# Combining two contraction tiles at a time: 512 KB loads and 512-wide vector steps beside a saturated TensorE

## The chip, the core and the metric

The kernel runs on one core of a Trainium2 chip. The metric is the time of one execution in device microseconds. TensorE does the matrix products (PE in the rows, its weight loads PEld), VectorE (DVE) and ScalarE (ACT) do elementwise work, GpSimd (POOL) issues the loads that add into their target, and SyncE (SP) issues nearly all other loads, in one queue that is worked off in order. Each engine executes its own list of instructions strictly in order.

## The reference

A decoder trunk of two layers over 512 tokens with 1024 features in float32. Each layer is, cut to what matters here:

```python
h = rmsnorm(x, norm_g)
proj = h @ w_in                      # feeds four token mixers, their gates and merge_in
...
merge = merge_in.reshape(B, T, N_BRANCH, D_MODEL)
for i, o in enumerate((o_nsa, o_pool, o_conv, o_fox)):
    branch = (o * silu(gates[:, :, i])) @ w_branch[i]
    acc += sigmoid(merge[:, :, i]) * branch
x = x + acc @ w_out
```

## The kernel before

Every float32 operand is split into a high and a low part in a reduced float32 format (`split`, line 69: ACT writes the high part, DVE subtracts it for the low part), and a product is three matmuls: high by high, low by high, high by low. Weights come as tiles of 128x1024 (512 KB); SP loads them one after the other into a small number of slots, `Stream` (line 97) hands them out in one fixed order, and `split` turns a tile into `wh` and `wl`, of which there are two buffers each. A `dense` (line 283) is one such tile against all eight tiles of the normed input: 24 matmuls.

A layer goes through these stages: projections, then attention (twelve units of four query blocks, with `dense` work between them to fill PE), then `branches(m)` for m = 0 to 3, each followed by four `dense` that compute merge logits (dense A to D of that `m` in this text), then `merge`, then the output projection. The merge logits of the other half of the features are computed in `merge` by a scheme with seven products in place of eight (`PRODUCTS`): the product of the two halves of the contraction and the two halves of the tokens is formed from combinations of the blocks. The combined weights are added up by accumulating loads and DVE. The combined inputs are made by `combine_h` (line 850) from x, which is read again from DRAM: the quarter pairs of contraction tile k and k + 4 are loaded, scaled by the norm's gain on ACT (line 867), and combined on DVE into P7, P6 and P3, which are then split. `combine_h` is a generator. Its steps are taken one at a time from within the dense work after the branches (lines 1218 to 1230), and the rest of it at the product P7 in `merge`.

Three buffers matter. `ptc` (2 buffers of 128x512) first holds the compressed probabilities of the attention, and then the x tiles of `combine_h`. `rope` (1 buffer of 128x2x512) holds the rotary tables and then two decay rows of the attention; from `more` (line 137) on it is one more slot for a merge weight, beside three slots cut from the attention's value tile `V` and the three ordinary `wr` slots.

The program order above is not the final one: when the kernel is built, a scheduler of the language reorders the instructions of each engine, by its own model of how long things take. So `combine_h` starts in the middle of the attention, and a change in one place moves instructions in others.

Of the kernel before, what the change touches and what calls it, by code (L numbers as in the profile page):

```python
# [9 lines left out]
F32R = mybir.dt.float32r  # L10
AF = mybir.ActivationFunctionType
ALU = mybir.AluOpType
# [4 lines left out]
T = 512  # L17
# [27 lines left out]
def trunk_kernel(ctx: ExitStack, tc: tile.TileContext, xT, w_all, par_all, const, gains, rope, outT):  # L45
    nc = tc.nc
    PE, ACT, DVE, POOL = nc.tensor, nc.scalar, nc.vector, nc.gpsimd
# [9 lines left out]
    def sb(shape, tag, bufs, dt=F32):  # L57
        return work.tile(shape, dt, tag=tag, name=tag, bufs=bufs)

    def temp():  # L60
        return sb([128, T], "t", 8)

    def psum(tag, bufs):
        return ps.tile([128, T], F32, tag=tag, name="ps_" + tag, bufs=bufs)
# [4 lines left out]
    def split(hi, lo, src, scale=None):  # L69

        if scale is None:
            ACT.activation(hi, src, AF.Copy)  # L72
            DVE.tensor_tensor(lo, src, f32(hi), ALU.subtract)  # L73
        else:
            ACT.activation(hi, src, AF.Copy, scale=scale)  # L75
            DVE.scalar_tensor_tensor(lo, src, scale, f32(hi), op0=ALU.mult, op1=ALU.subtract)  # L76
# [4 lines left out]
    ng = cpool.tile([128, 24], F32, name="ng")  # L81
# [11 lines left out]
    class Stream:  # L93
# [43 lines left out]
        def more(self):  # L137

            big = sb([128, 3, 1024], "V", 1)
            self.slots += ["rope"] + [big[:, n] for n in range(3)]  # L140
            self.fill()

        def next_raw(self):
# [73 lines left out]
    ws = Stream()  # L217
# [36 lines left out]
    def stats(n=T, keep=False):  # L254
        sum_squares(n, False, True)
        p = state["ssq"]
        nt = n // 128
        rt = sb([128, 4], "rtok", 2)
        DVE.tensor_scalar(rt[:, :nt], p[:, 0:nt], 1.0 / DM, 1e-6, op0=ALU.mult, op1=ALU.add)
        POOL.tensor_tensor(rt[:, :nt], rt[:, :nt], nhalf[:, :nt], ALU.pow)  # L260
        p2 = psum("o", 1)
        for tt in range(nt):
            PE.matmul(p2[:, tt * 128:tt * 128 + 128], rt[:, tt:tt + 1].to_broadcast([128, 128]), ident,
                      start=(tt == 0), stop=(tt == nt - 1))
        if keep:
            return rt, p2
        rb = sb([128, T], "rstd", 1)
        ACT.activation(rb, p2, AF.Copy)
        return rt, rb
# [220 lines left out]
    def cmp_attention():  # L490
        kc, vc, q, g = state["kc"], state["vc"], state["nq"], state["g"]
        pc = sb([128, 4, 4, 32], "p", 5)
        flat = pc.rearrange("p a h n -> p (a h) n")
        for half in range(2):
            p = psum("s", 2)
            for j in range(8):
                qt, h = half * 2 + j // 4, j % 4
                PE.matmul(p[:, j * 64:j * 64 + 64], q[h][:, qt * 128:qt * 128 + 128], kc,
                          start=(j == 0), stop=(j == 7))
            pv = p.rearrange("p (j two n) -> p j two n", two=2, n=32)  # L500
            t = temp()
            tv = t[:, 0:256].rearrange("p (j n) -> p j n", n=32)
            ACT.activation(tv, pv[:, :, 1, :], AF.Copy)
            yield
            DVE.tensor_tensor(flat[:, half * 8:half * 8 + 8, :], pv[:, :, 0, :], tv, ALU.add)
            yield
        for qt in range(4):
            m = cst[:, C_CM + qt * 32:C_CM + qt * 32 + 32].rearrange("p (o n) -> p o n", o=1)
            DVE.tensor_tensor(pc[:, qt], pc[:, qt], m.to_broadcast([128, 4, 32]), ALU.add)
        yield  # L510
        nm, sm = sb([128, 16], "cnm", 1), sb([128, 16], "csm", 1)
        DVE.tensor_reduce(nm, flat, axis=AX.X, op=ALU.min)

        def bc(a):
            return a.rearrange("p (a o) -> p a o", o=1).to_broadcast([128, 16, 32])

        yield
        DVE.tensor_tensor(flat, flat, bc(nm), ALU.subtract)
        ACT.activation(flat, flat, AF.Exp, scale=-1.0)
        yield  # L520
        DVE.tensor_reduce(sm, flat, axis=AX.X, op=ALU.add)
        DVE.reciprocal(sm, sm)
        DVE.tensor_tensor(sm.rearrange("p (a h) -> p a h", h=4), sm.rearrange("p (a h) -> p a h", h=4),
                          g[:, :, 0:4], ALU.mult)
        DVE.tensor_scalar(sm[:, 0:4], sm[:, 0:4], cst[:, C_VAL:C_VAL + 1], None, op0=ALU.mult)
        DVE.tensor_tensor(flat, flat, bc(sm), ALU.mult)
        yield
        yield
        pt = psum("pt", 2)
        for qt in range(4):  # L530
            PE.transpose(pt[:, qt * 128:qt * 128 + 128], pc[:, qt].rearrange("p h n -> p (h n)"), ident)
        ph, pl = sb([128, T], "ptc", 2, F32R), sb([128, T], "ptc", 2, F32R)
        split(ph, pl, pt)
        state["pc"] = (ph, pl)
        yield
# [314 lines left out]
    def combine_h(l):  # L850

        src = xT.rearrange("(k p) t -> k p t", p=128) if l == 0 else x1d
        H = T // 2
        S = state["S"] = {n: [] for n in ("P7", "P6", "P5", "P3")}
        lo_, hi_ = slice(0, H), slice(H, T)
        keep = []
        for k in range(4):
            xa = [sb([128, T], "ptc", 2) for _ in range(2)]
            for n in range(2):
                nc.sync.dma_start(xa[n], src[k + 4 * n])  # L860
            if k % 2 == 0:
                pair = {n: [sb([128, 2, H], "st", 20, F32R) for _ in range(2)] for n in ("P7", "P6", "P3")}
                s1 = sb([128, 2, H], "p", 5)
                keep.append(s1)
            yield
            for n in range(2):
                ACT.activation(xa[n], xa[n], AF.Copy, scale=ng[:, 8 * l + k + 4 * n:8 * l + k + 4 * n + 1])
            yield
            c = k % 2
            tmp = sb([128, 2, H], "p", 5)  # L870

            def parts(name, t):
                h, lo = (x[:, c] for x in pair[name])
                split(h, lo, t)
                S[name].append((h, lo))

            DVE.tensor_tensor(tmp[:, 0], xa[0][:, lo_], xa[0][:, hi_], ALU.subtract)
            DVE.tensor_tensor(s1[:, c], xa[1][:, hi_], xa[0][:, hi_], ALU.subtract)
            parts("P7", tmp[:, 0])
            yield  # L880
            DVE.scalar_tensor_tensor(tmp[:, 1], s1[:, c], -1.0, xa[0][:, lo_], op0=ALU.mult, op1=ALU.subtract)
            parts("P6", tmp[:, 1])
            yield
            s4 = xa[1][:, lo_]
            DVE.scalar_tensor_tensor(s4, s4, -1.0, tmp[:, 1], op0=ALU.mult, op1=ALU.subtract)
            parts("P3", s4)
            yield

        for k in range(4):
            h, lo = xh[k][:, hi_], xl[k][:, hi_]  # L890
            split(h, lo, keep[k // 2][:, k % 2])
            S["P5"].append((h, lo))
            yield
# [163 lines left out]
    for k in range(KT):  # L1057
        t = temp()
# [31 lines left out]
    for l in range(L):  # L1090
# [97 lines left out]

        fill = filler()
        side = itertools.chain(decay(l), cmp_attention())  # L1190
        for n in range(48):
            next(fill)
# [23 lines left out]

        ah, al = [], []
        side = combine_h(l)
        steps = 20
        for m in range(4):  # L1220
            if m == 1:
                ws.more()
# [62 lines left out]
    for half in range(2):  # L1285
        c = slice(half * T // 2, half * T // 2 + T // 2)
# [3 lines left out]
        _, rb = stats(T // 2, keep=True)  # L1290
        x = xn[KT - 1][:, c]
# [3 lines left out]
        for m in range(KT):  # L1295
            x = xn[m][:, c]
# [134 lines left out]
```

## Time and profile before

| what | value |
|---|---|
| median of 3 runs | 954.5 us (954.34 to 955.58) |
| profiled execution | 954.59 us, its span 952.8 us |
| TensorE busy | 933.3 us, 98% of the span |
| VectorE busy | 714.3 us, 75% |
| ScalarE busy | 520.2 us, 55% |
| mean DMA rate | 131 GB/s |

The profiled execution's time is 1.8 us more than its span, which goes from the first to the last instruction in the trace. Busy shares are averages over stages. The granted TensorE clock was 0.998 of full speed over the run, so the clock plays no part here.

### The profile page before, as it was taken

The numbers are of one execution on the slowest core, as the hardware profiler recorded it, in microseconds if no ns is written. First come the engines' busy times: TensorE is split into PE (matmuls) and PEld (weight loads), VectorE is DVE, ScalarE is ACT, GpSimd is POOL, SyncE is SP. The second block draws the span as 40 slices with busy tenths as digits, with TensorE's granted clock in tenths as the row PEclk, the third lists the DMA queues.
The fourth block names the chain that finished last, engine by engine and source line by source line (L and its number), as shares of the span: only waits on it lengthen the run. The fifth ranks groups of instructions, "written<-read, shape, count | busy, mean of one in ns | idle before, by whom it ended". The sixth has DMA issues, their size and how long they took to land.

```text
span 952.8 us, 12820 instructions
## 1 busy us (share of the span) xinstructions
PE 933.3 (98%) x4680; PEld 792.0 (83%) x4680; DVE 714.3 (75%) x1392; ACT 520.2 (55%) x906; POOL 31.1 (3%) x45
## 2 busy tenths in 40 slices
PE   7999999999999999999999999999999999999996
PEld 5988888888877888887889888888888788888796
DVE  6695689986887977776668548999777887686765
ACT  6295475575545454544426636656665455546273
POOL 0000000000000000000000000000000000010002
PEclk9999999999999999999999999999999999999999
DMA  6253122222136667643515421221322566685353
GB/s 267 79 161 127 67 89 67 79 89 89 67 122 167 176 202 217 177 155 130 192 64 162 142 89 67 89 67 47 110 67 78 179 166 187 198 208 199 112 166 122
DMA packets 39614, 124.73 MB, mean 131 GB/s; under 512 B 4464, under 2 KB 6528, under 8 KB 39552
## 3 DMA queue, kind: packets, MB, share of 16 engines
q1 hardware_dynamic: 35712, 112.38, 35.8%
q0 software_dynamic: 2976, 10.50, 5.7%
q10 hardware_dynamic: 864, 1.05, 0.3%
q8 instruction: 36, 0.59, 0.3%
q14 instruction: 26, 0.21, 0.1%
HBM read 119.72 MB, written 4.19 MB: 130 GB/s over the span
## 4 chain that ended last, share of the span: by engine, by line
PE 96%; DVE 2%; ACT 1%; DMA 1%; issue 0%; POOL 0%; DVEq 0%; SPq 0%; ACTq 0%; POOLq 0%
PE ps_d L303 56%; PE ps_d L988 9%; PE ps_s L988 5%; PE ps_o L698 3%; PE ps_pt L676 3%; PE ps_pt L988 2%; PE ps_pt L1026 2%; PE ps_s L554 2%; PE ps_pt L554 2%; PE ps_s L832 2%; PE ps_s L653 2%; PE ps_s L652 1%; PE ps_pt L832 1%; PE ps_o L1026 1%; PE ps_d L1026 1%; PE ps_o L415 1%
## 5 line engine op out<-in xcount | busy, mean ns | idle before, releaser
L303 PE MATMUL ps_d<-xh,wh 128*128 128x512 f32 x632 | 250.3, 397 | 9.0 <-ACT xh L75 6.8
L303 PE MATMUL ps_d<-xl,wh 128*128 128x512 f32 x632 | 250.2, 396 | 0.0
L72 ACT ACTIVATE wh<-wr 128x1024 fp32r<-128x1024 f32 (+2 forms) x134 | 138.9, 1038 | 155.2 <-PE ps_d L303 71.5
L73 DVE TENSOR_TENSOR wl<-wr,wh 128x1024 fp32r<-128x1024 f32 (+2 forms) x134 | 160.4, 1199 | 54.1 <-ACT wh L72 52.2
L303 PE MATMUL ps_d<-xh,wl 128*128 128x512 f32 x632 | 174.1, 392 | 0.0
L303 PEld LDWEIGHTS ps_d<-xh,wh 128*128 128x128 f32 x632 | 119.9, 190 | 32.9 <-ACT xh L75 6.8
L303 PEld LDWEIGHTS ps_d<-xl,wh 128*128 128x128 f32 x632 | 119.5, 189 | 23.8 <-DVE xl L76 1.2
L303 PEld LDWEIGHTS ps_d<-xh,wl 128*128 128x128 f32 x632 | 117.5, 188 | 23.1
L657 ACT ACTIVATE p<-p,nm 128x128 f32<-128x128 f32 (+1 forms) x96 | 53.3, 556 | 35.4 <-DVE nm L655 35.2
L324 DVE TENSOR_TENSOR t<-ps_d,rstd 128x512 f32<-128x512 f32 x74 | 50.7, 686 | 26.7 <-PE ps_d L303 26.3
L655 DVE CUSTOM_DVE_ANT_0 p<-ps_s,cst 128x128 f32<-128x128 f32 (+1 forms) x96 | 45.6, 484 | 13.0 <-PE ps_s L653 6.8
L72 ACT ACTIVATE ptx<-ps_pt 128x384 fp32r<-128x384 f32 (+1 forms) x72 | 37.0, 522 | 23.2 <-PE ps_o L698 14.4
L698 PE MATMUL ps_o<-ptx,V 128*128 128x256 f32 (+1 forms) x288 | 48.8, 282 | 0.6 <-DVE ptx L73 0.6
L698 PEld LDWEIGHTS ps_o<-ptx,V 128*128 128x128 f32 x288 | 42.4, 190 | 3.6 <-DVE ptx L73 0.8
L73 DVE TENSOR_TENSOR ptx<-ps_pt,ptx 128x384 fp32r<-128x384 f32 (+1 forms) x72 | 42.0, 593 | 2.1 <-ACT ptx L72 2.0
L676 PE MATMUL ps_pt<-cst,p 128*128 128x128 f32 x240 | 40.1, 276 | 0.0
L303 PE MATMUL ps_d<-y,wh 128*128 128x256 f32 (+1 forms) x176 | 38.0, 336 | 0.9 <-ACT y L75 0.9
L303 PE MATMUL ps_d<-st,wh 128*128 128x256 f32 (+1 forms) x176 | 33.5, 332 | 0.0
L72 ACT ACTIVATE wh<-V 128x1024 fp32r<-128x1024 f32 x18 | 19.1, 1061 | 22.7 <-PE ps_s L832 7.2
L303 PEld LDWEIGHTS ps_d<-y,wh 128*128 128x128 f32 x176 | 27.9, 190 | 4.2 <-ACT y L75 1.4
L73 DVE TENSOR_TENSOR wl<-V,wh 128x1024 fp32r<-128x1024 f32 x18 | 22.0, 1223 | 12.5 <-ACT wh L72 12.5
L676 PEld LDWEIGHTS ps_pt<-cst,p 128*128 128x128 f32 x240 | 28.1, 140 | 3.3
(341 smaller groups left out, 1726.1 us busy)
## 6 DMA issues: line engine op xcount, KB each, us to landing
wr<-in_w_all_dram SPq DMA_DIRECT2D x143, 512.0 KB, 3.3
V<-in_w_all_dram SPq DMA_DIRECT2D x26, 512.0 KB, 4.1
rope<-in_w_all_dram SPq DMA_DIRECT2D x12, 512.0 KB, 4.5
t<-in_xT_dram SPq DMA_DIRECT2D x16, 256.0 KB, 4.6
V<-in_w_all_dram POOLq DMA_DIRECT2D x8, 512.0 KB, 8.0
wr<-in_w_all_dram SPq DMA_DIRECT2D x8, 400.0 KB, 3.1
wr<-in_w_all_dram POOLq DMA_DIRECT2D x6, 512.0 KB, 6.1
ptc<-in_xT_dram SPq DMA_DIRECT2D x8, 256.0 KB, 2.9
```

The source lines that it names most:

```text
L72: ACT.activation(hi, src, AF.Copy)
L73: DVE.tensor_tensor(lo, src, f32(hi), ALU.subtract)
L303: PE.matmul(acc[:, :width], w, r[k][:, tok], start=(n == 0), stop=(n == 23))
L324: DVE.tensor_tensor(t, acc, state["rb"], ALU.mult)
L554: PE.matmul(accs[tt][:, 0:400], x[:, tt * 128:tt * 128 + 128], w, start=(k == 0 and a == 0), stop=(kp == 3 and kk == 1 and a == 2))
L655: DVE.tensor_tensor_reduce(out=P[:, :n], in0=s[:, :n], in1=bias, scale=1.0, scalar=3e38, op0=ALU.add, op1=ALU.min, accum_out=nm)
L657: ACT.activation(P[:, :n], P[:, :n], AF.Exp, bias=nm, scale=-1.0, accum_out=sm)
L676: PE.transpose(p[:, c:c + 128], self.P[qt][:, kb * 128:kb * 128 + 128], ident)
L698: PE.matmul(dst, V[:, kb, self.vset, :], part[:, src], start=(self.fresh and self.cmp is None and b == 0 and kb == 0 and j == 0), stop=(se ...
L832: PE.matmul(p, w[:, c], r, start=(n == 0), stop=(n == 5))
L988: PE.matmul(bank[tt], x, w[:, d], start=(opens and k == 0 and n == 0), stop=(name in ("P2", "P3", "P4") and k == 3 and n == 2), skip_group ...
L1026: PE.matmul(p, x[:, c], w[:, d], start=(n == 0), stop=(n == 5))
```

## The change

`combine_h` works on two contraction tiles at a time. It loads x tiles 2c and 2c + 1 (and 2c + 4 and 2c + 5) with one DMA of 512 KB each: the first pair goes to `ptc`, which becomes one buffer of 128x2x512, and the second to `rope`. The gains remain eight ACT instructions of 128x512 per layer, now two in a row on the same buffer. The combinations and their splits become half as many, each over 128x2x256, so 512 elements wide. The last combination is written to a scratch tile and no longer into the loaded one. `rope` is given to the merge weights only when `combine_h` ends, and not in `more`. The number of steps taken beside the dense work goes from 20 to 16.

```diff
--- before.py
+++ after.py
@@ -137,7 +137,7 @@
         def more(self):
 
             big = sb([128, 3, 1024], "V", 1)
-            self.slots += ["rope"] + [big[:, n] for n in range(3)]
+            self.slots += [big[:, n] for n in range(3)]
             self.fill()
 
         def next_raw(self):
@@ -529,7 +529,8 @@
         pt = psum("pt", 2)
         for qt in range(4):
             PE.transpose(pt[:, qt * 128:qt * 128 + 128], pc[:, qt].rearrange("p h n -> p (h n)"), ident)
-        ph, pl = sb([128, T], "ptc", 2, F32R), sb([128, T], "ptc", 2, F32R)
+        both = sb([128, 2, T], "ptc", 1, F32R)
+        ph, pl = both[:, 0], both[:, 1]
         split(ph, pl, pt)
         state["pc"] = (ph, pl)
         yield
@@ -854,37 +855,39 @@
         S = state["S"] = {n: [] for n in ("P7", "P6", "P5", "P3")}
         lo_, hi_ = slice(0, H), slice(H, T)
         keep = []
-        for k in range(4):
-            xa = [sb([128, T], "ptc", 2) for _ in range(2)]
+        for c in range(2):
+            xa = [sb([128, 2, T], tag, 1) for tag in ("ptc", "rope")]
             for n in range(2):
-                nc.sync.dma_start(xa[n], src[k + 4 * n])
-            if k % 2 == 0:
-                pair = {n: [sb([128, 2, H], "st", 20, F32R) for _ in range(2)] for n in ("P7", "P6", "P3")}
-                s1 = sb([128, 2, H], "p", 5)
-                keep.append(s1)
+                nc.sync.dma_start(xa[n], src[2 * c + 4 * n:2 * c + 4 * n + 2].rearrange("k p t -> p k t"))
+            pair = {n: [sb([128, 2, H], "st", 20, F32R) for _ in range(2)] for n in ("P7", "P6", "P3")}
+            s1, tmp, s2 = (sb([128, 2, H], "p", 5) for _ in range(3))
+            keep.append(s1)
             yield
             for n in range(2):
-                ACT.activation(xa[n], xa[n], AF.Copy, scale=ng[:, 8 * l + k + 4 * n:8 * l + k + 4 * n + 1])
-            yield
-            c = k % 2
-            tmp = sb([128, 2, H], "p", 5)
+                for e in range(2):
+                    k = 2 * c + e + 4 * n
+                    ACT.activation(xa[n][:, e], xa[n][:, e], AF.Copy, scale=ng[:, 8 * l + k:8 * l + k + 1])
+                yield
 
             def parts(name, t):
-                h, lo = (x[:, c] for x in pair[name])
+                h, lo = pair[name]
                 split(h, lo, t)
-                S[name].append((h, lo))
-
-            DVE.tensor_tensor(tmp[:, 0], xa[0][:, lo_], xa[0][:, hi_], ALU.subtract)
-            DVE.tensor_tensor(s1[:, c], xa[1][:, hi_], xa[0][:, hi_], ALU.subtract)
-            parts("P7", tmp[:, 0])
-            yield
-            DVE.scalar_tensor_tensor(tmp[:, 1], s1[:, c], -1.0, xa[0][:, lo_], op0=ALU.mult, op1=ALU.subtract)
-            parts("P6", tmp[:, 1])
-            yield
-            s4 = xa[1][:, lo_]
-            DVE.scalar_tensor_tensor(s4, s4, -1.0, tmp[:, 1], op0=ALU.mult, op1=ALU.subtract)
-            parts("P3", s4)
-            yield
+                S[name] += [(h[:, e], lo[:, e]) for e in range(2)]
+
+            DVE.tensor_tensor(tmp, xa[0][:, :, lo_], xa[0][:, :, hi_], ALU.subtract)
+            parts("P7", tmp)
+            yield
+            DVE.tensor_tensor(s1, xa[1][:, :, hi_], xa[0][:, :, hi_], ALU.subtract)
+            yield
+            DVE.scalar_tensor_tensor(s2, s1, -1.0, xa[0][:, :, lo_], op0=ALU.mult, op1=ALU.subtract)
+            parts("P6", s2)
+            yield
+            DVE.scalar_tensor_tensor(tmp, xa[1][:, :, lo_], -1.0, s2, op0=ALU.mult, op1=ALU.subtract)
+            parts("P3", tmp)
+            yield
+            yield
+        ws.slots.append("rope")
+        ws.fill()
 
         for k in range(4):
             h, lo = xh[k][:, hi_], xl[k][:, hi_]
@@ -1216,7 +1219,7 @@
 
         ah, al = [], []
         side = combine_h(l)
-        steps = 20
+        steps = 16
         for m in range(4):
             if m == 1:
                 ws.more()
```

Lines of the changed kernel are one to three higher than before from line 532 on (the scaling of line 867 stands at 869, `o` of line 721 at 722).

The first place is ACT at the end of the attention of layer 0, from the first split of the last head's probabilities (`ptx<-ps_pt`) to the weights of the first two merge logits' tiles (`wh<-wr`). `o` is the output of a head as it leaves PSUM, `ptc` an x tile being scaled. Before:

```order
L72 ACTIVATE ptx<-ps_pt 128x384 x2
L72 ACTIVATE wh<-wr 128x1024
L721 ACTIVATE o<-ps_o 64x512
L72 ACTIVATE ptx<-ps_pt 128x512
L867 ACTIVATE ptc<-ptc,ng 128x512
L72 ACTIVATE ptx<-ps_pt 128x384
L721 ACTIVATE o<-ps_o 64x512
L817 ACTIVATE t<-t 128x512
L709 ACTIVATE y<-o 128x512
L72 ACTIVATE ptx<-V 128x1024
L817 ACTIVATE t<-t 128x512
L72 ACTIVATE wh<-wr 128x1024 x2
```

And now:

```order
L72 ACTIVATE ptx<-ps_pt 128x384 x2
L72 ACTIVATE wh<-wr 128x1024
L869 ACTIVATE ptc<-ptc,ng 128x512 x2
L722 ACTIVATE o<-ps_o 64x512
L72 ACTIVATE ptx<-ps_pt 128x512
L72 ACTIVATE ptx<-ps_pt 128x384
L722 ACTIVATE o<-ps_o 64x512
L818 ACTIVATE t<-t 128x512
L710 ACTIVATE y<-o 128x512
L818 ACTIVATE t<-t 128x512
L72 ACTIVATE ptx<-V 128x1024
L72 ACTIVATE wh<-wr 128x1024 x2
```

Two scalings stand now ahead of the head's output and of the last two splits, where one stood behind the first of these.

The second place is ACT during the four dense of m = 0 in layer 0, from the weights of dense C to those of the tile after dense D. `t` is a merge logit, `st` a high part of a combination. Before:

```order
L72 ACTIVATE wh<-wr 128x1024
L817 ACTIVATE t<-t 128x512
L867 ACTIVATE ptc<-ptc,ng 128x512
L72 ACTIVATE wh<-wr 128x1024
L817 ACTIVATE t<-t 128x512
L72 ACTIVATE st<-p 128x256
L72 ACTIVATE st<-ptc 128x256
L867 ACTIVATE ptc<-ptc,ng 128x512
L72 ACTIVATE st<-p 128x256
L72 ACTIVATE wh<-wr 128x1024
```

And now:

```order
L72 ACTIVATE wh<-wr 128x1024
L869 ACTIVATE rope<-rope,ng 128x512 x2
L818 ACTIVATE t<-t 128x512
L72 ACTIVATE wh<-wr 128x1024
L818 ACTIVATE t<-t 128x512
L72 ACTIVATE st<-p 128x512 x2
L72 ACTIVATE wh<-wr 128x1024
```

The weights of dense D (the second `wh<-wr`) stand behind two scalings in place of one, and behind the logit.

The third place is the queue of SP in layer 1, from the middle of the attention to the merge weights. `x1d` is the input of layer 1 in DRAM. Before:

```order
L170 DMA rope<-in_w_all_dram 128x1024
L170 DMA wr<-in_w_all_dram 128x1024
L860 DMA ptc<-x1d 128x512 x2
L170 DMA wr<-in_w_all_dram 128x1024 x5
L860 DMA ptc<-x1d 128x512
L170 DMA wr<-in_w_all_dram 128x1024 x2
L170 DMA V<-in_w_all_dram 128x1024 x4
```

And now:

```order
L861 DMA rope<-x1d 128x2x512
L170 DMA wr<-in_w_all_dram 128x1024
L861 DMA ptc<-x1d 128x2x512
L170 DMA wr<-in_w_all_dram 128x1024 x6
L861 DMA ptc<-x1d 128x2x512
L170 DMA wr<-in_w_all_dram 128x1024
L170 DMA V<-in_w_all_dram 128x1024 x4
L170 DMA wr<-in_w_all_dram 128x1024 x2
L861 DMA rope<-x1d 128x2x512
L170 DMA wr<-in_w_all_dram 128x1024 x2
L170 DMA rope<-in_w_all_dram 128x1024
```

`rope` gets x tiles and its first merge weight only after the second pair of them, and one weight load in place of two stands between the third load of x and those into `V`.

## Rows read from the trace of the kernel before

**Rows 1.** The page: span, and part 1, busy time and instructions of TensorE.
```profile
span 952.8 us, 12820 instructions
...
PE 933.3 (98%) x4680; PEld 792.0 (83%) x4680; DVE 714.3 (75%) x1392; ACT 520.2 (55%) x906; POOL 31.1 (3%) x45
```

**Rows 2.** Waits of PE: releaser: us in total, times, longest.
```profile
PE ps_d L303 <- ACT xh L75: 6.8, 1, 6.8
PE ps_d L303 <- ACT wh L72: 2.1, 2, 1.6
PE ps_s L832 <- DVE y L711: 1.1, 2, 0.9
```

**Rows 3.** Windows of layer 0: stretch, busy time by engine, clock, DMA share, GB/s.
```profile
264.00:292.00 28.00, 26.53 (x132) 21.42 (x131) 25.36 (x41) 12.32 (x19) 0.64 (x1) 1.00 0.36 126
292.00:330.00 38.00, 38.00 (x170) 31.46 (x169) 31.04 (x55) 20.99 (x37) 2.02 (x3) 1.00 0.68 180
330.00:428.00 98.00, 98.00 (x433) 80.89 (x432) 72.04 (x81) 50.10 (x61) 4.30 (x5) 1.00 0.64 187
```

**Rows 4.** Timeline of PE, both layers: start, us, operation, idle before it.
```profile
271.37 0.49 PE L676 MATMUL ps_pt<-cst,p 128*128 128x128 f32 x3
...
303.44 0.39 PE L303 MATMUL ps_d<-xh,wh 128*128 128x512 f32 x1
303.67 0.39 PE L303 MATMUL ps_d<-xl,wh 128*128 128x512 f32 x1
...
751.86 0.50 PE L303 MATMUL ps_d<-xh,wh 128*128 128x512 f32 x1 [1.60 <-ACT wh L72]
...
768.31 0.39 PE L303 MATMUL ps_d<-xh,wh 128*128 128x512 f32 x1
```

**Rows 5.** Timeline of ACT, both layers.
```profile
275.34 0.72 ACT L867 ACTIVATE ptc<-ptc,ng 128x512 f32<-128x512 f32 x1 [0.31 <-DMA ptc<-in_xT_dram]
...
284.40 1.06 ACT L72 ACTIVATE ptx<-V 128x1024 fp32r<-128x1024 f32 x1 [0.94 <-DMA V<-in_w_all_dram]
...
300.06 0.72 ACT L867 ACTIVATE ptc<-ptc,ng 128x512 f32<-128x512 f32 x1 [2.73 <-DMA ptc<-in_xT_dram]
300.69 1.04 ACT L72 ACTIVATE wh<-wr 128x1024 fp32r<-128x1024 f32 x1
...
749.28 1.06 ACT L72 ACTIVATE ptx<-V 128x1024 fp32r<-128x1024 f32 x1 [2.01 <-DMA V<-in_w_all_dram]
...
763.85 0.73 ACT L867 ACTIVATE ptc<-ptc,ng 128x512 f32<-128x512 f32 x1 [1.64 <-DMA ptc<-x1d]
```

**Rows 6.** Timeline of the loads that SP issues, both layers.
```profile
272.67 0.33 SPq L860 DMA_DIRECT2D ptc<-in_xT_dram  x1
...
279.71 8.18 SPq L170 DMA_DIRECT2D V<-in_w_all_dram  x4
...
294.97 0.33 SPq L860 DMA_DIRECT2D ptc<-in_xT_dram  x1
...
734.47 7.44 SPq L170 DMA_DIRECT2D wr<-in_w_all_dram  x2
743.56 8.39 SPq L170 DMA_DIRECT2D V<-in_w_all_dram  x4
...
759.03 0.33 SPq L860 DMA_DIRECT2D ptc<-x1d  x1
```

**Rows 7.** Groups by form, ACT then DVE: count, busy us, mean ns of one.
```profile
L867 ACT ACTIVATE ptc<-ptc,ng 128x512 f32<-128x512 f32 x16 | 11.4, 720 | 10.1 <-DMA ptc<-in_xT_dram 5.5 <-DMA ptc<-x1d 4.5
...
L72 ACT ACTIVATE st<-p 128x256 fp32r<-128x256 f32 x16 | 6.1, 408 | 5.9 <-DVE p L881 4.8 <-DVE p L877 1.1
...
L75 ACT ACTIVATE st<-t 128x512 fp32r<-128x512 f32 x8 | 5.0, 624 | 14.2 <-DVE t L841 14.2
...
L841 DVE TENSOR_TENSOR t<-t 128x512 f32<-128x512 f32 x24 | 16.3, 685 | 0.1
...
L73 DVE TENSOR_TENSOR st<-p,st 128x256 fp32r<-128x256 f32 x16 | 6.4, 421 | 0.1
```

More of the change, by code (lines that the diff above doesn't have):

```diff
@@ L865, in combine_h @@
             yield
             for n in range(2):
-                ACT.activation(xa[n], xa[n], AF.Copy, scale=ng[:, 8 * l + k + 4 * n:8 * l + k + 4 * n + 1])
-            yield
-            c = k % 2
-            tmp = sb([128, 2, H], "p", 5)
-            def parts(name, t):
-                h, lo = (x[:, c] for x in pair[name])
-                split(h, lo, t)
-                S[name].append((h, lo))
-            DVE.tensor_tensor(tmp[:, 0], xa[0][:, lo_], xa[0][:, hi_], ALU.subtract)
-            DVE.tensor_tensor(s1[:, c], xa[1][:, hi_], xa[0][:, hi_], ALU.subtract)
@@ L879, in combine_h, with parts @@
-            parts("P7", tmp[:, 0])
+                for e in range(2):
+                    k = 2 * c + e + 4 * n
+                    ACT.activation(xa[n][:, e], xa[n][:, e], AF.Copy, scale=ng[:, 8 * l + k:8 * l + k + 1])
+                yield
+            def parts(name, t):
+                h, lo = pair[name]
+                split(h, lo, t)
+                S[name] += [(h[:, e], lo[:, e]) for e in range(2)]
+            DVE.tensor_tensor(tmp, xa[0][:, :, lo_], xa[0][:, :, hi_], ALU.subtract)
```

## The prediction

> **What bounds the kernel now.** I read the page's first part first: TensorE is busy in 98% of the span [rows 1]. A busy share of PE can hide matmuls that run at less than their rate, so I next looked at the step from one matmul to the next: two neighbours of 512 columns start 0.23 us apart in a dense tile [rows 4], and nearly all of the run is made of such steps. What is not PE at its rate is in the waits of PE [rows 2]: 6.8 us at the start of the program, where the first inputs arrive, and then very little: 2.1 us in two waits for weights (`wh`) and 1.1 us in two waits for the last head's `y`. The windows say where [rows 3]: in layer 0, 1.5 of the 28 us around the end of the attention are idle, and none of the 38 us in which the branches, their dense tiles and most of `combine_h` run, and none of the 98 us of `merge`, which uses the combinations. DVE is at 31.0 of 38 us and ACT at 21.0 of 38 there, so neither sets the pace. The change is thus made in stretches in which PE doesn't wait, and it can gain only where PE waits at the attention's end, or lose where its new order makes PE wait.
>
> **Less work on DVE and ACT.** Per layer 28 DVE operations of 256 elements (seven for each of four tiles) become 14 of 512. A split of 256 took 0.421 us, an addition of 512 took 0.685 us [rows 7]: 28 x 0.421 = 11.8 us becomes 14 x 0.685 = 9.6 us, 2.2 us less. On ACT 12 high parts at 0.408 us become 6 at 0.624 us [rows 7], 4.9 us to 3.7 us, 1.2 us less; the eight scalings stay at 0.72 us each. PE was idle for nothing in that window [rows 3], so these 3.4 us per layer are worth 0 on the path. The one place where DVE holds PE is the chain that makes `y` of the last head, and in neither order does an operation of `combine_h` stand in that chain. I take 0; a gain from it is a rival below.
>
> **The two scalings at the attention's end, layer 0.** Now they stand on ACT ahead of the last outputs of the heads, in a queue that PE waits for. Before, the load was issued at 272.67 and its scaling began at 275.34, after a wait of 0.31 us for it [rows 5, 6]: 2.67 us for 256 KB. In the change the DVE operation that frees `ptc` stands behind one more split, and it and the combination before it are 0.26 us longer each (0.685 against 0.421 us [rows 7]): I put the issue at about 274.0, an estimate. Landing in 2.67 us, it is there at 276.7, and two scalings of 0.72 us end at 278.1. Does `o` wait for that? PE ends the last head's first transposes at about 271.6 [rows 4]. In the changed order there stand 27 matmuls of 512 columns between these and the ones that end the head before, which `o` reads, where the old order had few; at 0.23 us, with about 0.8 us of small ones, they end at 278.5. So `o` isn't late: the scheduler put dense work there. There is 0.4 us of slack, and then another 13 or so matmuls (2.1 us, against 1.3 us that ACT and DVE take to empty `o`, at 0.62 and 0.69 us [rows 7]) that give 0.8 us more. The load may land in 2.67 + 0.4 + 0.8 = 3.9 us before PE waits; above that each us costs one. Bounds: 0 at 2.67 us; 1.2 us at 5.1 us, the landing in the busier stretch below. The bytes double, but they go in rows of the same size and the queue is nearly empty here, so I take 0. In layer 1 the scalings stand behind `o` and one more split, which leaves more slack: 0.
>
> The Trainium skill, in DMA: Bandwidth & Descriptors, section Anatomy of one DMA, gives about 2.0 us fixed and then bytes at 436 GB/s, an estimate of 2.6 us for 256 KB and 3.2 us for 512 KB. The first agrees with 2.67 us here, and by the second the tail would be free as well. But the same load in the branches took 5.09 us, so a sum by that rule would leave out the next term and come out 0.7 us lower.
>
> **The second load of `rope`, in front of dense D.** In layer 0 the load of 294.97 was first used at 300.06, after a wait of 2.73 us [rows 5, 6]: 5.09 us, while weight loads and an accumulating load were under way and the DMA engines were at 0.68 [rows 3]. In layer 1 it was 759.03 to 763.85, 4.82 us. Behind that wait stand the weights of dense D: `wh` at 300.69, done at 301.73, and PE took them at 303.44 [rows 4, 5]. From landing to PE's start there were 3.38 us in layer 0 and 768.31 - 763.85 = 4.46 us in layer 1. Now the chain from landing is two scalings, a logit and the weights: 0.63 + 0.72 + 0.62 + 1.04 = 3.0 us; in layer 1 a high part more, 0.55 us. The load is issued some 0.4 us later, since three wider operations precede it. And it is 512 KB: the other 256 KB cost between 0 (two of them may share the queue) and 1.46 us (256 KB at the 180 GB/s of that window); I take 0.6. Layer 0: 3.0 + 0.4 + 0.6 - 3.38 = **+0.6 us** (0 to 1.5). Layer 1: 3.0 + 0.55 + 0.4 + 0.6 - 4.46 = **+0.1 us** (0 to 1.0). The low part on DVE is needed 14 matmuls (3.2 us) later and isn't late. Behind the scalings on ACT wait the logit, nobody's bound, and the weights of the tile after D, which had 2 us to spare.
>
> **One weight load fewer ahead of V, layer 1.** In layer 0 the first of the merge weights into `V` was issued at 279.71, and ACT could split the third at 284.40: 4.7 us. In layer 1, 743.56 to 749.28: 5.7 us, and there two weight loads had been issued between 734.47 and 741.9, where layer 0 had one [rows 5, 6]. ACT waits for that split ahead of the weights of dense A, for which PE waited 1.60 us [rows 4]; by subtraction from the total of 2.1 us it was 0.5 us in layer 0 [rows 2]. The changed queue has one load there. If that is the reason, layer 1 gains up to 1.1 us; if not, 0. I take half: **-0.5 us**.
>
> **The order at the end of layer 1.** The wait for `y` was 0.9 us once and 0.2 us once [rows 2]. Layer 1 now has the order that layer 0 had. I take **+0.3 us** (0 to 0.7).
>
> **The merge weights.** `rope` held a merge weight early, and now gets it after the second pair of x. SP's queue stands at that load until the last combination has read `rope`, about 10 us after 294.97; the weights behind it wait for their own slots until then anyway. In `merge`, PE idled for nothing [rows 3], and seven slots are filled well before it starts at 330: 0. If the cover were gone, it would be one load of 512 KB, 3 to 5 us per layer.
>
> **Reordered attention.** The scheduler moved instructions over the second half of the attention in both layers. The matmuls are the same; a new wait there can't be read from an order. 0, with 0.6 us to either side.
>
> **Sum:** 0.6 + 0.1 - 0.5 + 0.3 = +0.5 us, to 954.59 + 0.5 = 955.1 us for the profiled execution. The median of the runs is 0.1 us under that execution, so I forecast **955.0 us**: no change, by 0.2% (1.9 us), which is about what a measurement of this kernel can tell from none.
>
> **Rivals.** (1) *Slower: the large loads hold ACT.* If 512 KB land as slowly as the branches' rows suggest, the tail of layer 0 costs 1.2 us and the two dense D 1.5 and 1.0 us: with +0.3 and -0.5 it is 954.5 + 3.5 = 958.0 us. For it: two waits of 2.73 and 1.64 us for loads half as large [rows 5]. Against it: slack at three of the four loads per layer. It decides when the extra 256 KB cost over 1.2 us and the tail's load takes over 4.5 us. The Trainium skill speaks for this side: Perfetto Trace Analysis, section DMA Optimizations, says that where DMA engines are mostly idle, smaller transfers may let part of the work start sooner; here the first scaling used to start after 256 KB. Chance 0.20.
> (2) *Faster: DVE and ACT relief ends PE's waits.* If the 3.2 us of waits for `wh` and `y` [rows 2] go, it is 951.3 us; half of that is not yet told from no change. For it: these are the only waits and they stand next to the changed work. Against it: the chain behind them has no instruction of `combine_h` in it, and the `wh` wait is a landing. Chance 0.13.
> (3) *Late merge weights*, 3 to 5 us per layer, 961 to 964 us. Against it: no wait of PE in 98 us [rows 3]. Chance 0.02.
> The forecast, within 0.2%, has 0.65.
>
> **How the numbers follow.** Faster 0.13, same 0.65, slower 0.22. The range leaves out about half of each outer case: from 952.6, the edge of the faster case, which holds part of it, to 957.4, between the upper end of my terms (0.6 us of reordering, 1.5 and 1.0 us at dense D) and rival 1.
>
> **What would show it.** After the change, ACT's scalings of `rope` before dense D wait 2.5 to 4 us for a load, and PE has a wait for `wh` there of under 1 us; DVE's busy time falls by about 4 us in all and ACT's by 2 to 3, with PE's busy time and rate unchanged; the split of `V` in layer 1 starts less than 5.5 us after its load's issue; PE idles for nothing in `merge`. I am wrong if a wait of several us stands on PE behind `ptc` or `rope`, if `merge` shows waits for loads, or if PE's waits around the attention's end vanish.

## The result and the profile after

The changed kernel takes 961.01 us (median of 6 runs, 959.77 to 966.85) against 954.59 us (953.81 to 955.58): a ratio of 1.007 [1.0053, 1.0088], so 6.4 us slower. The forecast of no change was wrong, and the time lies above its range. The profiled execution of the change took 959.82 us with a span of 957.9 us, 5.1 us more than the span in [rows 1]. By time it is the second shortest of the six; no trace shows what the longer ones lost on top.

The page: span and first part.

```profile
span 957.9 us, 12770 instructions
...
PE 935.1 (98%) x4680; PEld 792.7 (83%) x4680; DVE 710.9 (74%) x1364; ACT 518.7 (54%) x894; POOL 31.1 (3%) x45
```

DVE works 3.4 us less and ACT 1.5 us less, where the prediction's terms make 4.4 and 2.4 us over both layers, for the same 4680 matmuls. So most of the relief came, and did not help.

PE is busy for 1.8 us more than before, and idle for 3.3 us more (957.9 - 935.1 = 22.8 us against 952.8 - 933.3 = 19.5 us): together the 5.1 us of the span.

The waits of PE after: releaser, us in total, times, longest. They answer to [rows 2].

```profile
PE ps_d L303 <- ACT xh L75: 6.7, 1, 6.7
PE ps_d L303 <- ACT wh L72: 3.4, 2, 1.9
PE ps_s L833 <- DVE y L712: 1.8, 2, 0.9
PE ps_o L699 <- DVE o L723: 1.1, 1, 1.1
...
PE ps_s L833 <- DVE wl L73: 0.7, 2, 0.5
```

The waits for `wh` have grown by 1.3 us, those for `y` by 0.7 us; behind `o` (1.1 us) and `wl` (0.7 us) there are new ones. That is 3.8 us of waits; smaller ones that came and went leave the 3.3 us of idle time. All four stand where the attention ends and dense A begins, and `merge` has none, as the windows of layer 0 say (columns as in [rows 3]; then two short ones of layer 1):

```profile
264.00:292.00 28.00, 23.94 (x118) 18.92 (x117) 21.86 (x34) 13.29 (x20) 0.00 (x0) 1.00 0.37 132
292.00:330.00 38.00, 38.00 (x168) 31.25 (x167) 28.15 (x40) 16.67 (x26) 2.26 (x3) 1.00 0.58 167
330.00:428.00 98.00, 98.00 (x433) 80.84 (x433) 71.55 (x79) 50.10 (x61) 4.68 (x6) 1.00 0.67 188
...
751.50:755.10 3.60, 1.44 (x5) 0.92 (x6) 3.60 (x6) 2.62 (x4) 0.00 (x0) 1.00 0.07 26
755.10:758.50 3.40, 3.40 (x9) 2.61 (x9) 3.40 (x5) 2.32 (x4) 0.00 (x0) 0.52 0.48 154
```

The second of these stretches in the kernel before:

```profile
755.10:758.50 3.40, 3.40 (x17) 2.82 (x16) 3.30 (x7) 2.19 (x6) 0.93 (x1) 1.00 0.83 200
```

Where [rows 3] had 1.5 us idle in 28, there are now 4.1. The two short windows of the change show something that a table of waits can't: in layer 1 PE is busy for 1.44 of 3.60 us, and the granted clock of the 3.4 us behind them is 0.52. That is the lower of its two levels, 1.2 GHz. Before the change the clock was at 1.00 in the same stretch, with 17 matmuls begun in place of 9. The timeline of PE in the change:

```profile
751.80 0.50 PE L833 MATMUL ps_s<-y,wh 128*128 128x512 f32 x1 [0.89 <-DVE y L712]
...
754.85 0.49 PE L303 MATMUL ps_d<-xh,wh 128*128 128x512 f32 x1 [1.85 <-ACT wh L72]
...
755.53 0.63 PE L303 MATMUL ps_d<-xh,wh 128*128 128x512 f32 x1
755.96 0.63 PE L303 MATMUL ps_d<-xl,wh 128*128 128x512 f32 x1
...
758.83 0.40 PE L303 MATMUL ps_d<-xh,wh 128*128 128x512 f32 x1
759.06 0.40 PE L303 MATMUL ps_d<-xl,wh 128*128 128x512 f32 x1
```

After the two waits the matmuls start 0.43 us apart in place of 0.23. From 755.53 to 758.83 that is eight steps in 3.30 us, the last one partly at the old rate, where eight of 0.23 us are 1.84 us: 1.5 us lost, with PE busy all the time, so that no table of waits holds it. That is most of the 1.8 us by which PE's busy time grew.

What is behind the waits for `wh` stands in ACT's timeline (compare [rows 5]):

```profile
273.72 1.34 ACT L869 ACTIVATE ptc<-ptc,ng 128x512 f32<-128x512 f32 x2 [0.93 <-DMA ptc<-in_xT_dram]
275.08 0.59 ACT L722 ACTIVATE o<-ps_o 64x512 f32<-64x512 f32 x1
...
286.38 1.06 ACT L72 ACTIVATE ptx<-V 128x1024 fp32r<-128x1024 f32 x1 [0.63 <-DMA V<-in_w_all_dram]
287.34 1.99 ACT L72 ACTIVATE wh<-wr 128x1024 fp32r<-128x1024 f32 x2
...
302.13 1.34 ACT L869 ACTIVATE rope<-rope,ng 128x512 f32<-128x512 f32 x2 [3.77 <-DMA rope<-in_xT_dram]
...
752.80 1.06 ACT L72 ACTIVATE ptx<-V 128x1024 fp32r<-128x1024 f32 x1 [0.98 <-DMA V<-in_w_all_dram]
753.76 1.99 ACT L72 ACTIVATE wh<-wr 128x1024 fp32r<-128x1024 f32 x2
```

and in SP's loads (compare [rows 6]):

```profile
267.32 0.33 SPq L170 DMA_DIRECT2D wr<-in_w_all_dram  x1
268.85 0.38 SPq L861 DMA_DIRECT2D ptc<-in_xT_dram  x1
...
280.20 9.37 SPq L170 DMA_DIRECT2D V<-in_w_all_dram  x4
...
295.73 0.38 SPq L861 DMA_DIRECT2D rope<-in_xT_dram  x1
...
746.26 9.37 SPq L170 DMA_DIRECT2D V<-in_w_all_dram  x4
```

ACT splits a merge weight from `V` into `ptx` ahead of the weights of dense A and B. From the issue of the first load into `V` to the start of that split it was 4.69 us and 5.72 us before [rows 5, 6]; now it is 286.38 - 280.20 = 6.18 us and 752.80 - 746.26 = 6.54 us. I took the reason from `prepare`, which puts every third merge weight in `ptx`, so the first time the third. When `rope` took the first one early, the third was the second load into `V`. Now `rope` holds x tiles, and the third weight is the third load into `V`. That the later split makes the waits for `wh`, and these the fall of the clock, is **theory 1**. **Theory 2** is the first rival of the prediction: the 512 KB loads with two scalings behind them hold ACT.

### The profile page after: what moved, and what is told of

Its sections match the earlier page's. It is cut to its first block, busy times and chain, and to the rows that moved or that the text cites. A ratio compares the mean times of both kernels' runs of the same rounds, so it can differ in the third digit from the quotient of the medians.

```text
span 957.9 us, 12770 instructions
## 1 busy us (share of the span) xinstructions
PE 935.1 (98%) x4680; PEld 792.7 (83%) x4680; DVE 710.9 (74%) x1364; ACT 518.7 (54%) x894; POOL 31.1 (3%) x45
## 4 chain that ended last, share of the span: by engine, by line
PE 95%; DMA 2%; DVE 1%; ACT 1%; issue 1%; SPq 0%; POOL 0%; DVEq 0%; ACTq 0%; POOLq 0%
PE ps_d L303 55%; PE ps_d L991 9%; PE ps_s L991 5%; PE ps_o L699 3%; PE ps_pt L677 3%; PE ps_pt L1029 2%; PE ps_pt L991 2%; PE ps_s L555 2%; PE ps_pt L555 2%; PE ps_s L833 2%; PE ps_s L654 2%; PE ps_s L653 1%; PE ps_pt L833 1%; PE ps_d L1029 1%; PE ps_o L1029 1%; DMA V<-in_w_all_dram 1%
## 5 line engine op out<-in xcount | busy, mean ns | idle before, releaser
L72 ACT ACTIVATE wh<-wr 128x1024 fp32r<-128x1024 f32 (+2 forms) x136 | 141.2, 1040 | 176.9 <-PE ps_d L303 80.5
L73 DVE TENSOR_TENSOR wl<-wr,wh 128x1024 fp32r<-128x1024 f32 (+2 forms) x136 | 162.7, 1199 | 56.5 <-ACT wh L72 56.2
L72 ACT ACTIVATE wh<-V 128x1024 fp32r<-128x1024 f32 x20 | 21.2, 1059 | 30.6 <-PE ps_pt L1029 10.6
L654 PE MATMUL ps_s<-st 128*128 128x128 f32 (+1 forms) x96 | 30.5, 324 | 0.0
```

The costliest lines, as they stand in the source:

```text
L654: PE.matmul(s[:, :n], q2[:, c], kl[:, :n], start=False, stop=True)
```

## Experiments

Times are medians beside runs of the kernel before on the same chip, with the ratio and its interval.

**The lost slot alone.** The kernel before, with nothing changed but when `rope` is handed over (behind the last P3 of `combine_h`):

```diff
-            self.slots += ["rope"] + [big[:, n] for n in range(3)]
+            self.slots += [big[:, n] for n in range(3)]
...
+        ws.slots.append("rope")
+        ws.fill()
```

> The kernel before with one part of the change alone: `rope` is given to the merge weights when `combine_h` ends, not in `more`. Theory 1 (the merge tile that `prepare` puts in `ptx`, the third, becomes the third load into `V` instead of the second, lands later and holds ACT ahead of the weights of dense A and B): PE's waits for `wh` at the start of dense A grow from 0.5 and 1.6 us to about 1.5 and 1.9 us, 955.9 us, and some us more if the granted clock falls behind the wait as it does in the change. Theory 2 (the 512 KB loads with their two scalings hold ACT): the waits and the time stay, 954.6 us.

958.9 us against 953.91, 1.0055 [1.0043, 1.0067]. In 256 KB loads and 256-wide operations, this one line costs 5.0 us. PE's waits for `wh` are those of the change and more, and PE's timeline of layer 0 shows the half clock behind them, a window of layer 1 too:

```profile
PE ps_d L303 <- ACT wh L72: 4.0, 2, 2.1
```

```profile
285.07 0.50 PE L832 MATMUL ps_s<-y,wh 128*128 128x512 f32 x1 [0.90 <-DVE y L711]
288.18 0.50 PE L303 MATMUL ps_d<-xh,wh 128*128 128x512 f32 x1 [1.92 <-ACT wh L72]
288.99 0.63 PE L303 MATMUL ps_d<-xl,wh 128*128 128x512 f32 x1
289.41 0.63 PE L303 MATMUL ps_d<-xh,wh 128*128 128x512 f32 x1
```

```profile
756.50:759.90 3.40, 3.40 (x10) 2.65 (x9) 3.40 (x5) 1.86 (x5) 0.58 (x1) 0.52 0.55 173
```

In the profiled execution the waits for `wh` grew by 1.9 us, and the clock fell in both layers, at about 1.5 us each: 4.9 us, of 5.2 us by which its span of 958.0 us exceeds that of [rows 1]. This bears theory 1 out, and the clock is the larger part of the loss. The execution is the longest of the five (960.08 us, mean clock 0.993); three of the others have a mean clock of 0.996, and no trace shows how their loss is made up.

**The size of the loads alone.** The change with two loads of 256 KB in place of each of 512 KB:

```diff
-                nc.sync.dma_start(xa[n], src[2 * c + 4 * n:2 * c + 4 * n + 2].rearrange("k p t -> p k t"))
+                for e in range(2):
+                    nc.sync.dma_start(xa[n][:, e], src[2 * c + 4 * n + e])
```

> The changed kernel, with each 512 KB load of x made as two of 256 KB, everything else of the change kept. In its order the two scalings of the attention's end stand behind the last head's `o` but one in both layers. Theory 2 (size of the loads, ACT held by them): PE's wait of 1.1 us behind `o` in layer 0 goes, and most of the loss with it, 956 us. Theory 1: only that 1.1 us goes, the waits for `wh` stay at 1.5 and 1.9 us, 958.7 to 960 us.

960.4 us, 1.0068 [1.0056, 1.008]. The wait behind `o` is gone from PE's waits, and those for `wh` are 4.0 us. Theory 2 as the main cause is out; the 1.1 us behind `o` were real, but can't be told apart in the time, since the waits for `wh` grew by 0.6 us and the clock fell in both layers of the profiled execution, not in one. ACT's scalings in layer 0:

```profile
274.36 1.32 ACT L870 ACTIVATE ptc<-ptc,ng 128x512 f32<-128x512 f32 x2
```

The rule on smaller transfers that the prediction set on that side (the Trainium skill, Perfetto Trace Analysis, DMA Optimizations) is left untested by this: the scalings also stand behind `o` in this order, and waited for no load there, as the row shows.

**The split's tile loaded first.** `count % 3 == 0` in place of `== 2` in `prepare`, on either kernel, so that the tile which is split early is the first load into `V` in the change, and the one in `rope` in the kernel before.

> The changed kernel, with the first and not the third of each three merge tiles put in `ptx`, so that the tile which ACT splits ahead of dense A is the first load into `V`. Theory 1: the waits for `wh` fall from 1.5 and 1.9 us to under 0.6 us each, and without them the clock stays at its upper level in layer 1: 957 us (959.8 less 2.3 us of waits, and less 1.7 us if the clock goes with them, 956 us). Theory 2: the wait for `V` isn't what holds PE, the time stays at 960 to 961 us.

> The kernel before, with the first and not the third of each three merge tiles put in `ptx`: that is the tile which lies in `rope` long before. Theory 1: ACT's split waits for no load, PE's two waits for `wh` (2.1 us in all) go, 952.5 us. Rival (the weights of dense A wait for PE's release of `wh` or for `y` anyway): 954.6 us, no change.

961.29 us, 1.0079 [1.0066, 1.0092], and 960.93 us, 1.007 [1.0058, 1.0082]. In the profiled executions the waits for `wh` fell as expected, to 0.6 us and 0.5 us, but the time did not. PE's waits of the second kernel, and its DVE at the end of layer 1:

```profile
PE ps_s L832 <- DVE y L711: 3.2, 2, 1.6
...
PE ps_d L303 <- ACT wh L72: 0.5, 1, 0.5
```

```profile
745.61 1.22 DVE L73 TENSOR_TENSOR ptx<-rope,ptx 128x1024 fp32r<-128x1024 f32 x1
746.74 0.68 DVE L324 TENSOR_TENSOR t<-ps_d,rstd 128x512 f32<-128x512 f32 x1
747.46 0.68 DVE L722 TENSOR_TENSOR o<-ps_o,o 64x512 f32<-64x512 f32 x1
```

With its tile there early, the scheduler puts the split into the chain that makes `y` of the last head: its low part, 1.22 us, stands ahead of `o` on DVE. PE now waits for `y`, 1.6 us in each layer, and the half clock comes back in one of them. The wait was moved, not taken away. This execution, at 958.37 us, is the shortest of its five; the others are 2.1 to 3.4 us longer, and no trace shows by what. In the changed kernel the high part stands ahead of `y` on ACT, and waits there for its load into `V` (1.69 and 1.57 us), so PE's waits for `y` grow in the same way. The expectation was wrong in taking the rest of the order as given.

**The split taken away from that place.** Here the third weight goes to `wh` and `wl` and only later thirds to `ptx` (`count % 3 == 2 and n > 2`), so it is split when `merge` begins. Four kernels:

> The changed kernel, with the third merge tile put in `wh` and `wl` and the later thirds in `ptx` as before, so that in ACT's order no split of a load into `V` stands ahead of the weights of dense A, and nothing else there is moved. Theory 1 (that split, late by its load, makes the waits for `wh`, and the waits together pull the clock down): PE's 3.4 us of waits for `wh` go, the clock keeps its upper level there, and what stays over the kernel before is the 1.1 us behind `o` and some tenths behind `y` and `wl`: 954.0 to 955.5 us. Theory 2 (512 KB loads on ACT): 958 us or more.

> The same edit on the kernel before. Theory 1: its 2.1 us of waits for `wh` go, 952.0 us (0.2% faster). Rival, as with the first tile in `ptx`, which only moved the waits: something else (the tile's own load, `y`) ends at the same time and takes their place, 953.9 us or more.

> The changed kernel with the third merge tile in `wh` and `wl`, and each 512 KB load of x made as two of 256 KB, by which the scalings stand behind `o` at the attention's end. If the waits for `wh` and the one behind `o` are all that the change loses, it is at or under the kernel before: 952.5 to 953.9 us. If the wider operations or the place of the x loads cost something of their own, 955 us or more.

> The kernel before, with `rope` given to the merge weights when `combine_h` ends, and the third merge tile in `wh` and `wl`. Theory 1: a late `rope` slot costs something only through the split ahead of dense A: with that gone the 5.0 us that it cost go too, 952.0 us, as the same edit with `rope` early. Rival (the slot was needed for the merge weights themselves, or a lost slot slows the loads): 954 us or more, with waits of PE in `merge`.

971.21 us (1.0176 [1.0158, 1.0195]), 963.68 us (1.0097 [1.0082, 1.0113]), 970.31 us (1.0169 [1.0154, 1.0185]) and 974.25 us (1.021 [1.0187, 1.0232]): all far slower, and what theory 1 forecast was wrong in all four. The rival of the last one, late merge weights with waits of PE in `merge`, came. The waits for `wh` at dense A did go, to 0.9 us in each of the four. But `merge`, in which PE had idled for nothing, now starts with waits. In the first of these kernels, PE's waits, one row of ACT, and the loads of SP:

```profile
PE ps_d L991 <- ACT wh L72: 6.6, 2, 3.8
...
PE ps_d L991 <- DVE wl L73: 2.2, 2, 1.4
```

```profile
334.50 1.06 ACT L72 ACTIVATE ptx<-wr 128x1024 fp32r<-128x1024 f32 x1 [7.45 <-DMA wr<-in_w_all_dram]
```

```profile
280.05 1.28 SPq L170 DMA_DIRECT2D V<-in_w_all_dram  x3
...
327.82 16.16 SPq L170 DMA_DIRECT2D V<-in_w_all_dram  x4
```

Without the early split no load into `V` is issued between 281.3 and 327.8 us (before, the row of [rows 6] had four, the last behind the split; now three). The weights behind it come late, and ACT waits 7.45 us for one. So the slot that the early split sets free is what keeps `merge` supplied, and its wait for `V` is the price of that.

**The split kept early, off ACT and DVE.** The third weight's two parts are made on GpSimd:

```diff
+            if n == 2:
+                POOL.tensor_copy(hi, r)
+                POOL.tensor_tensor(lo, r, f32(hi), ALU.subtract)
+            else:
                 split(hi, lo, r)
```

> The changed kernel, with both parts of the third merge tile, high and low, made on GpSimd into `ptx` and not on ACT and DVE; ACT's other instructions at the attention's end keep their order. The early split is kept, so `merge` should start without waits, and ACT doesn't wait for V any more. Theory 1: the waits for `wh` at dense A fall from 3.4 to 0.9 us, the clock stays at its upper level in layer 1, and 1.1 us behind `o` and some tenths behind `y` and `wl` stay: 955 to 956 us, against 961.0. Theory 2 (512 KB loads on ACT are what costs): 958.5 us or more.

> The same edit on the kernel before. Theory 1: its waits for `wh` fall from 2.1 to 0.9 us, no wait in `merge`: 952.5 to 953 us, against 954.2. Rival: GpSimd's two operations are so long, or so late, that `merge` waits for the third tile: 955 us or more, with waits of PE at the start of `merge`.

> The changed kernel with the third merge tile split on GpSimd and each 512 KB load of x made as two of 256 KB, by which the scalings stand behind `o`. If the waits for `wh` and the one behind `o` are the whole loss of the change, 953.5 to 954.8 us, level with the kernel before. If batching costs something else, 956 us or more.

> The kernel before with `rope` given to the merge weights when `combine_h` ends (which alone cost 5.0 us), and the third merge tile split on GpSimd. Theory 1: the late slot costs only through the wait of ACT's split for its load, so nothing of the 5.0 us is left: 953.8 us, as with the early slot and the same split. Rival (the late slot also makes merge weights late, or slows other loads): 955.5 us or more, with waits of PE in `merge`.

The change: 956.94 us, 1.0028 [1.0018, 1.0039], so by the ratios 4.0 us of its loss are gone; that is 0.9 us above what theory 1 expected. The kernel before: 953.79 us, 0.9993 [0.9984, 1.0002]; theory 1 expected a gain of 1.2 to 1.7 us, and the 0.7 us by this ratio can't be told from none. The change with 256 KB loads: 955.26 us, 1.0017 [1.0008, 1.0025], between the two cases of its expectation, and by the ratios 1.0 us under the first of these kernels, about as much as the wait behind `o` that it lacks, though the intervals overlap. The kernel before with the late slot: 956.12 us beside 954.62, 1.001 [0.9995, 1.0024], where the slot alone had cost 1.0055. PE's waits in the first of them:

```profile
PE ps_s L833 <- DVE y L712: 1.8, 2, 0.9
PE ps_d L303 <- ACT wh L72: 1.6, 4, 0.5
...
PE ps_o L699 <- DVE o L723: 0.9, 1, 0.9
PE ps_s L833 <- DVE wl L73: 0.7, 2, 0.5
```

No wait for `wh` is over 0.5 us, and in the profiled runs of all four the clock stays at 1.00 from 10 to 930 us. So the wait of ACT for `V` carries most of what the late slot costs. The edit also takes 1.06 us of ACT's and 1.23 us of DVE's work out of this place; that this alone counts for little is seen in the kernel before, which gains 0.7 us by its ratio. A part stays open: with this split the late slot takes 1.001 where the early one takes 0.9993, about 1.6 us of the 5.0 us by the ratios. Its median, 956.12 us, is where the rival was expected, but the profiled execution has no wait in `merge`. Single runs took 953.4 to 958.7 us, seven of the twelve over 955.5 us, and the profiled one, at 953.58, doesn't show what the long ones waited for.

**The batching without the lost slot.** The second pair of x tiles in a buffer of its own (`ptd`, paid for by 18 `st` buffers in place of 20), `rope` in `more` again; then the same with the GpSimd split; and the kernel before with 18 `st` buffers as control.

```diff
-            xa = [sb([128, 2, T], tag, 1) for tag in ("ptc", "rope")]
+            xa = [sb([128, 2, T], tag, 1) for tag in ("ptc", "ptd")]
```

> The changed kernel with a buffer of its own for the second pair of x tiles (paid for by 18 instead of 20 `st` buffers), and `rope` given to the merge weights in `more` as before the change: the 512 KB loads and the wide operations without the loss of the slot. Theory 1: the split ahead of dense A has its load as early as before the change, waits for `wh` of 2 to 2.5 us, no fall of the clock: 954 to 956 us. Theory 2: 958 us or more, with the waits of the change.

> The changed kernel with a buffer of its own for the second pair of x tiles (18 `st` buffers), the early `rope` slot, and the third merge tile split on GpSimd: all of the batching, none of the lost slot, and no wait of ACT for `V`. If batching itself gains, by DVE's and ACT's relief, it is under 952.8 us; if it is worth nothing, 953 to 954.5 us, level with the kernel before; if it costs, as the 1.4 us that were left with two loads of 256 KB and this split may say, 955 us or more.

> The kernel before with 18 instead of 20 `st` buffers and nothing else: the control for the kernels with a buffer of their own. If the two `st` buffers don't matter, 953.9 us; if giving them up costs, 955 us or more, and the batching in those kernels is better by the same amount.

954.74 us, 1.0012 [0.9998, 1.0026]; 953.91 us, 0.9989 [0.9979, 0.9999]; control 954.65 us, 1.0001 [0.9991, 1.0011]. With the slot back, 512 KB loads and 512-wide operations cost nothing that can be told from the control. The second kernel is under the kernel before and the change, by 0.1%, about as much as the kernel before gains from the GpSimd split, and at the edge of what could be told. The first's single runs go from 952.6 to 959.9 us, and its profiled one is the longest: it has the waits for `wh` (4.0 us) and the fall of the clock that theory 1 had not expected there. Its loads and ACT in layer 1:

```profile
742.71 0.33 SPq L170 DMA_DIRECT2D V<-in_w_all_dram  x1
743.13 0.39 SPq L170 DMA_DIRECT2D wr<-in_w_all_dram  x1
743.57 10.78 SPq L170 DMA_DIRECT2D V<-in_w_all_dram  x3
```

```profile
751.68 1.06 ACT L72 ACTIVATE ptx<-V 128x1024 fp32r<-128x1024 f32 x1 [4.46 <-DMA V<-in_w_all_dram]
```

Here a weight for `wr` was put between the first and the second load into `V`, so the third merge weight was again third in a row; the split came 9.0 us after the first issue, and PE waited 3.5 us. It is the same kind of wait, but the place alone does not make it: the order of the queue is the same in all twelve runs, and six of them took under 954.7 us. What made this landing so late is not shown.

The control's profiled execution, 957.21 us and the longest of its twelve, shows that the kernel before stood near this edge. In layer 1 its split, second in line as in the kernel before, started 6.07 us after the first issue, and PE waited 1.96 us:

```profile
752.37 0.50 PE L303 MATMUL ps_d<-xh,wh 128*128 128x512 f32 x1 [1.96 <-ACT wh L72]
```

The half clock followed (0.57 over 753 to 757 us). Of the 80 runs of the kernel before beside the experiments, eight have a mean clock of 0.994 or 0.995 and took 955.5 to 957.6 us; the other 72, at 0.996 to 0.998, took 952.9 to 955.6 us.

## Why the prediction was wrong, step by step

**The step that failed is "The merge weights ... 0".** It asked whether the weights that `rope` had held would be late for `merge`, and [rows 3] answered rightly that they would not: PE idles for nothing there after the change too. But it had not followed the one weight that ACT takes before `merge`. [rows 5] showed that split with its waits for `V` of 0.94 and 2.01 us, and the order showed `rope` missing from its early place; I did not put the two together. The lost slot alone measured 5.0 us, and with the slot kept the batching measured 1.0012 with an interval that holds 1. Through ACT's wait for `V` go about 3.4 us of the 5.0; the path of the rest is open.

**"One weight load fewer ahead of V, -0.5 us" had the wrong sign,** by the same omission. The split in layer 1 came 6.54 us after the first issue, not under 5.5 us: more loads into `V` stood ahead of its own. With its tile first (the change with the first tile in `ptx`), second (the kernel before) and third in line (the change), the split started 3.29 us, 5.72 us and 6.54 us after the first issue in layer 1, each time behind a wait for `V`. Whether the weight load that went made a difference beside that was not tried.

**The price of a wait was too low.** Each us of idle PE was priced as one us. In the change the two waits of layer 1 were followed by 1.5 us lost at half clock, and the mean granted clock was 0.989 to 0.994 in its six runs, against 0.998 in the profiled run before. The text ahead of the prediction said that the clock plays no part, from a run in which it hadn't fallen, and the prediction took PE's rate as unchanged.

**The attention's end, layer 0:** the mechanism was right and the size off. The threshold was a landing of 3.9 us, above which each us costs one. The load of 268.85 was used at 273.72, 4.87 us, so a cost of about 1.0 us; PE's wait behind `o` was 1.1 us. The load was issued 5 us earlier than I had put it, but PE ended the last head's first transposes 6 us earlier too (265.3, not 271.6), so the threshold nearly held. I had taken 2.67 us from the load half as large, with the queue nearly empty; but here a weight load had been issued 1.5 us ahead (267.32), where before the nearest was 7.4 us ahead (265.26 to 272.67). No run separates this from the size. The upper bound of the term, 1.2 us at 5.1 us, was nearly it.

By the estimate from the Trainium skill (DMA: Bandwidth & Descriptors, Anatomy of one DMA) the 512 KB would have been there after 3.2 us. The section gives its fit for loads that GpSimd issues, and SP issued this one. This trace shows 4.87 us here, and 302.13 - 295.73 = 6.40 us for the load in the branches.

**Dense D:** the forecast was +0.6 and +0.1 us, with a wait of ACT of 2.5 to 4 us. In layer 0 ACT's wait came (3.77 us), but no wait of PE behind it: dense A itself had begun 1.5 us later, which gave the slack back. In layer 1 the order wasn't the one that the term took: the weights of dense D (767.76 us on ACT) stand ahead of the scalings of `rope` (768.71), which waited for nothing.

**`y` in layer 1:** +0.3 forecast; by its waits +0.7, the upper bound. **Relief of DVE and ACT, 0:** right, as far as the kernels with the slot kept can tell. **Reordered attention, 0 with 0.6 us to either side:** the new waits for `wl`, 0.7 us, and one of 0.3 us came, and one of 0.6 us went, 0.4 us in all.

**The rivals.** The first named the right sign and its place at the attention's end, but the loads of x are about 1.1 us of the loss. The third, late merge weights, was the right family: a weight was late, in front of `merge` and not in it.

## What to carry to other kernels

When a buffer is handed over later, follow each thing that had used it early to its first reader, not to the stage that is named after it. A wait that sits in front of a saturated engine may have a reason: before taking it away, look for what the waiting instruction sets free (here a slot that feeds the next stage, worth more than the wait). Where the busiest engine's clock can fall, a wait is worth more than its length, and that part of the loss stands in the rate of the matmuls after it, not in any list of waits.

## What the runs showed of the hardware

- The granted clock fell to its lower level, 1.2 GHz, behind short waits: 0.89 and 1.85 us in layer 1 of the change, 0.90 and 1.92 us in layer 0 of the kernel with the slot alone. Behind 0.89 and 1.51 us in layer 0 of the change it stayed at the upper one, 2.4 GHz, as it did behind the 0.24 and 1.60 us of layer 1 before; behind 0.26 and 1.96 us in the control with 18 `st` buffers it fell. The matmuls started 0.43 us apart at the one level and 0.23 us at the other. What decides between such neighbours was not tried.
- Of a row of 512 KB loads into `V`, the first, second and third were used 3.3 to 3.4 us, 4.7 to 6.1 us, and 6.2 to 6.8 us after the first issue, each behind a wait for the load (first: the change with the first tile in `ptx`; second: the kernel before and the control; third: the change, the slot alone, the two 256 KB loads).
- GpSimd, which did nothing else there, took 1.04 to 1.55 us for the high part of a 128x1024 tile and 2.40 to 3.30 us for the low part in the profiled kernels with its split, by traces whose times on GpSimd are rough; on ACT and DVE it is 1.06 and 1.23 us. In the change, layer 0:

```profile
287.02 1.47 POOL L923 CAST ptx<-V 128x1024 fp32r<-128x1024 f32 x1 [79.53 <-DVE t L838]
288.58 2.41 POOL L924 TENSOR_TENSOR ptx<-V,ptx 128x1024 fp32r<-128x1024 f32 x1
```
